# Column mean of an 8192 x 8192 matrix: the running sum moved from VectorE to TensorE, with all loads on one queue and the last two tiles in pieces

## Chip, cores, metric

One core of one Trainium2 chip (trn2). The metric is device time in microseconds (us); a profile adds the span of one profiled execution, which is about 2 us shorter. In the profile lines PE is TensorE, PEld its weight loads, DVE VectorE, ACT ScalarE, SP SyncE, q a DMA queue. A load has landed when its last part has arrived.

## The reference

```python
def setup_inputs():
    return {"x": np.random.randn(8192, 8192).astype(np.float32)}

def reference(x):
    return np.mean(x, axis=0)
```

The input is 268.4 MB, the output 32 KB.

## The kernel before

Rows are cut into 64 tiles of 128 partitions x 8192 columns. VectorE keeps a running sum of the tiles; at the end TensorE sums over the partitions with a column of 1/8192.

```python
tiles = ctx.enter_context(tc.tile_pool(name="tiles", bufs=4))
# ... (cut: other pools)
nc.vector.memset(ones, 1.0 / R)
dma_engines = [nc.sync, nc.scalar]
for b in range(nb):                                   # 64 tiles
    t = tiles.tile([P, C], fdt, tag="xtile")
    dma_engines[b % 2].dma_start(out=t, in_=xb[b])    # two queues in turn
    if b == 0:
        prev = t
    elif b == 1:
        nc.vector.tensor_add(acc, prev, t)
    else:
        nc.vector.tensor_add(acc, acc, t)
for j in range(ng):                                   # 16 blocks of 512 columns
    ps = psum.tile([1, G], fdt, tag="ps")
    nc.tensor.matmul(out=ps, lhsT=ones, rhs=acc[:, j*G:(j+1)*G], start=True, stop=True)
    nc.scalar.copy(out=out_sb[:, j*G:(j+1)*G], in_=ps)
nc.sync.dma_start(out=out, in_=out_sb[0:1, :])
```

## Time and profile before

| | before |
|---|---|
| time, median of 15 runs | 663.13 us (662.15 to 664.72) |
| span of the profiled run | 660.1 us |
| loads | 432 GB/s until about 624 us, then nothing |
| VectorE | 64 instructions, 547.7 us busy; one addition 8.69 us |
| after VectorE's last wait for a load (623.2) | 36.9 us: two additions, 16 matmuls, copy, store |

The prediction below shows the lines. They are read in two stages: as long as the DMA share is 1.00, the loads set the pace, however busy VectorE is; after that the engines work one after the other, and every microsecond counts.

### The profile page before, as it was taken

Reading aid. Unit: us, or ns where it says so; the run is one execution under the profiler, and the core shown is the slowest. Engines: PE = TensorE matmul, PEld = TensorE weight load, DVE = VectorE, ACT = ScalarE, POOL = GpSimd, SP = SyncE. Lnnn points to the kernel's source line nnn. Section 1 sums busy time; section 2 is a strip of 40 time slices with the busy share of each in tenths; the row PEclk is TensorE's granted clock in tenths of the full one; section 3 lists DMA queues with packets and bytes.
Section 4 is the critical chain, followed back from the end, with each engine's and each line's share of the span. In section 5 each row is a group of like instructions: output and inputs, shape, how many; then the busy total and the mean of one; then the engine's idle time right before and its main releaser. Section 6 shows DMA issues by size and latency. Waiting matters only on the chain.

```text
span 660.1 us, 379 instructions
## 1 busy us (share of the span) xinstructions
PE 15.6 (2%) x32; PEld 2.8 (0%) x32; DVE 547.7 (83%) x64; ACT 10.5 (2%) x17; POOL 0.2 (0%) x4
## 2 busy tenths in 40 slices
PE   0000000000000000000000000000000000000017
PEld 0000000000000000000000000000000000000001
DVE  0548999888888988888988888898888899888880
ACT  0000000000000000000000000000000000000005
POOL 0000000000000000000000000000000000000000
PEclk9999999999999999999999999999999999999999
DMA  9999999999999999999999999999999999999700
GB/s 381 439 421 443 427 431 439 421 443 425 433 439 419 445 421 437 437 421 445 415 441 437 421 445 415 443 433 425 443 415 445 429 429 439 419 445 427 338 0 2
DMA packets 9220, 268.49 MB, mean 407 GB/s; under 512 B 1025, under 2 KB 1025, under 8 KB 1025
## 3 DMA queue, kind: packets, MB, share of 16 engines
q10 hardware_dynamic: 4608, 134.22, 47.3%
q1 hardware_dynamic: 4610, 134.25, 47.3%
q14 instruction: 2, 0.02, 0.0%
HBM read 268.44 MB, written 0.03 MB: 407 GB/s over the span
## 4 chain that ended last, share of the span: by engine, by line
DMA 74%; DVE 22%; PE 2%; issue 0%; ACT 0%; SPq 0%; DVEq 0%
DMA t<-in_x_dram 74%; DVE acc L49 22%; PE ps L55 2%; ACT out_sb L62 0%; SPq L43 0%; DVEq L49 0%
## 5 line engine op out<-in xcount | busy, mean ns | idle before, releaser
L49 DVE TENSOR_TENSOR acc<-acc,t 128x8192 f32<-128x8192 f32 x62 | 538.9, 8692 | 70.3 <-DMA t<-in_x_dram 69.3
L55 PE MATMUL ps<-acc,ones 128*1 128x512 f32 x32 | 15.6, 652 | 640.7 <-DVE acc L49 640.7
L47 DVE TENSOR_TENSOR acc<-t 128x8192 f32<-128x8192 f32 x1 | 8.7, 8693 | 21.9 <-DMA t<-in_x_dram 21.9
L62 ACT ACT_TABLE_LOAD x1 | 1.3, 1283 | 602.2 <-DVE acc L49 602.2
L62 ACT COPY out_sb<-ps 1x512 f32<-1x512 f32 x16 | 9.2, 575 | 44.3 <-PE ps L55 44.3
L55 PEld LDWEIGHTS ps<-acc,ones 128*1 128x1 f32 x32 | 2.8, 89 | 652.6 <-DVE acc L49 640.7
L35 DVE MEMSET ones<- 128x1 f32 x1 | 0.1, 59 | 0.8 <-PEq L79 0.8
L79 POOL MEMSET const-uint8-127<- 128x1 uint8 x1 | 0.1, 103 | 0.0
L79 POOL MEMSET const-bfloat16-1.0<- 128x1 bf16 x1 | 0.1, 102 | 0.0
L79 POOL MEMSET const-float32-0.0<- 128x1 f32 x1 | 0.1, 99 | 0.2 <-issue 0.2
L79 POOL MEMSET const-float32-1.0<- 128x1 f32 x1 | 0.1, 99 | 0.0
## 6 DMA issues: line engine op xcount, KB each, us to landing
t<-in_x_dram ACTq DMA_DIRECT2D x32, 4096.0 KB, 26.2
t<-in_x_dram SPq DMA_DIRECT2D x32, 4096.0 KB, 30.0
out_dram<-out_sb SPq DMA_DIRECT2D x1, 32.0 KB
```

Of the source, the lines that this page charges most:

```text
L35: nc.vector.memset(ones, 1.0 / R)
L47: nc.vector.tensor_add(acc, prev, t)
L49: nc.vector.tensor_add(acc, acc, t)
L55: nc.tensor.matmul(out=ps, lhsT=ones, rhs=acc[:, j * G : (j + 1) * G], start=True, stop=True,)
L62: nc.scalar.copy(out=out_sb[:, j * G : (j + 1) * G], in_=ps)
L79: nc = _bacc.Bacc("TRN2", target_bir_lowering=False, num_devices=1)
```

## The change

The intent is to remove the serial end. TensorE adds each tile straight into PSUM accumulators as it lands, neighbouring column blocks in different column groups (strips of TensorE's array, chosen by the output's first partition, here 0 and 64) and in different banks of PSUM. All loads go on one queue. The last two tiles come in 16 pieces of 1024 columns. ScalarE and VectorE share the copies, and half of the result is stored early.

```diff
-    acc = accp.tile([P, C], fdt)
-    dma_engines = [nc.sync, nc.scalar]
-        dma_engines[b % 2].dma_start(out=t, in_=xb[b])
-            nc.vector.tensor_add(acc, acc, t)
 ... (cut)
+    NBANK = 8
+    PSPART = [0, 64, 32, 96]
+    TAIL_TILES = 2
+    DW = 1024
+    def ps_ap(j):
+        s = j % 2                       # neighbours in different column groups
+        k = (j // 2 + 4 * s) % NBANK    # and in different banks
+        p = PSPART[s]
+        return ps_tiles[k][p : p + 1, :]
 ... (cut: emit_copy: even j on ScalarE, odd j on VectorE; emit_out: store one half)
+        if b < nb - TAIL_TILES:
+            nc.sync.dma_start(out=t, in_=xb[b])
+            for j in range(ng):
+                nc.tensor.matmul(out=ps_ap(j), lhsT=ones, rhs=t[:, j * G : (j + 1) * G],
+                                 start=(b == 0), stop=(b == nb - 1))
+        else:
+            for c in range(ndw):
+                nc.sync.dma_start(out=t[:, c * DW : (c + 1) * DW],
+                                  in_=xb[b][:, c * DW : (c + 1) * DW])
 ... (cut: the same matmuls piece by piece; copies and stores in the last tile)
```

More of the change, by code (lines that the diff above doesn't have):

```diff
@@ L5 @@
 import concourse.tile as tile
-from concourse import bass_utils, mybir
+from concourse import mybir
 from concourse._compat import with_exitstack
@@ L21 @@
     nb = R // P
-    xb = x.rearrange("(b p) c -> b p c", p=P)
-    fdt = mybir.dt.float32
-    tiles = ctx.enter_context(tc.tile_pool(name="tiles", bufs=4))
-    accp = ctx.enter_context(tc.tile_pool(name="accp", bufs=1))
-    consts = ctx.enter_context(tc.tile_pool(name="consts", bufs=1))
-    outp = ctx.enter_context(tc.tile_pool(name="outp", bufs=1))
-    psum = ctx.enter_context(tc.tile_pool(name="psum", bufs=4, space=bass.MemoryType.PSUM))
-    acc = accp.tile([P, C], fdt)
+    fdt = mybir.dt.float32
@@ new lines @@
+    G = 512
+    ng = C // G
+    assert C % G == 0
+    NBANK = 8
+    nsets = (ng + NBANK - 1) // NBANK
+    PSPART = [0, 64, 32, 96]
+    assert nsets <= len(PSPART)
+    TAIL_TILES = 2
+    DW = 1024
+    ndw = C // DW
+    xb = x.rearrange("(b p) c -> b p c", p=P)
+    tiles = ctx.enter_context(tc.tile_pool(name="xt", bufs=4))
+    consts = ctx.enter_context(tc.tile_pool(name="cst", bufs=1))
+    stag = ctx.enter_context(tc.tile_pool(name="stg", bufs=1))
+    psum = ctx.enter_context(tc.tile_pool(name="ps", bufs=1, space=bass.MemoryType.PSUM))
@@ L34 @@
     ones = consts.tile([P, 1], fdt)
     nc.vector.memset(ones, 1.0 / R)
-    out_sb = outp.tile([1, C], fdt)
-    dma_engines = [nc.sync, nc.scalar]
-    prev = None
-    for b in range(nb):
-        t = tiles.tile([P, C], fdt, tag="xtile")
-        dma_engines[b % 2].dma_start(out=t, in_=xb[b])
-        if b == 0:
-            prev = t
-        elif b == 1:
-            nc.vector.tensor_add(acc, prev, t)
-        else:
-            nc.vector.tensor_add(acc, acc, t)
-    G = 512
-    ng = C // G
@@ L53 @@
-    for j in range(ng):
-        ps = psum.tile([1, G], fdt, tag="ps")
-        nc.tensor.matmul(
-            out=ps,
-            lhsT=ones,
-            rhs=acc[:, j * G : (j + 1) * G],
-            start=True,
-            stop=True,
-        )
-        nc.scalar.copy(out=out_sb[:, j * G : (j + 1) * G], in_=ps)
-    nc.sync.dma_start(out=out, in_=out_sb[0:1, :])
+    nbank_used = min(NBANK, ng)
+    ps_tiles = [
+        psum.tile([P, G], fdt, tag=f"ps{k}", name=f"ps{k}")
+        for k in range(nbank_used)
+    ]
@@ new lines, in ps_ap, with emit_copy @@
+    def ps_ap(j):
[3 more added lines that the diff above has]
+        return ps_tiles[k][p : p + 1, :]
+    set_w = nbank_used * G
+    stage = stag.tile([max(PSPART[:nsets]) + 1, set_w], fdt)
+    outv = out.rearrange("(k s g) -> s k g", s=2, g=G)
+    def emit_copy(j):
+        p = PSPART[j % 2]
+        dst = stage[p : p + 1, (j // 2) * G : (j // 2 + 1) * G]
+        if j % 2 == 0:
+            nc.scalar.copy(out=dst, in_=ps_ap(j))
+        else:
+            nc.vector.tensor_copy(out=dst, in_=ps_ap(j))
@@ new lines, in emit_out @@
+    def emit_out(h):
+        half = set_w // 2
+        for s in range(nsets):
+            p = PSPART[s]
+            eng = nc.sync if s == 0 else nc.scalar
+            eng.dma_start(
+                out=outv[s : s + 1, h * 4 : (h + 1) * 4, :],
+                in_=stage[p : p + 1, h * half : (h + 1) * half].rearrange("p (k g) -> p k g", g=G),
+            )
+    for b in range(nb):
+        t = tiles.tile([P, C], fdt, tag="xt")
+        if b < nb - TAIL_TILES:
+            nc.sync.dma_start(out=t, in_=xb[b])
+            for j in range(ng):
+                nc.tensor.matmul(
+                    out=ps_ap(j),
+                    lhsT=ones,
+                    rhs=t[:, j * G : (j + 1) * G],
+                    start=(b == 0),
+                    stop=(b == nb - 1),
+                )
+        else:
+            per = DW // G
+            for c in range(ndw):
+                nc.sync.dma_start(
+                    out=t[:, c * DW : (c + 1) * DW],
+                    in_=xb[b][:, c * DW : (c + 1) * DW],
+                )
+            for c in range(ndw):
+                for jj in range(per):
+                    j = c * per + jj
+                    nc.tensor.matmul(
+                        out=ps_ap(j),
+                        lhsT=ones,
+                        rhs=t[:, j * G : (j + 1) * G],
+                        start=(b == 0),
+                        stop=(b == nb - 1),
+                    )
+                    if b == nb - 1:
+                        emit_copy(j)
+                if b == nb - 1 and c == ndw // 2 - 1:
+                    emit_out(0)
+            if b == nb - 1:
+                emit_out(1)
```

## The prediction

> **What bounds the kernel now.** I read the profile in this order: the totals of the page, then the chain of work that ended last, then the windows, then the timeline of the last 40 us. The totals alone mislead, because they show VectorE as the busiest engine:
>
> ```profile
> span 660.1 us, 379 instructions
> PE 15.6 (2%) x32; PEld 2.8 (0%) x32; DVE 547.7 (83%) x64; ACT 10.5 (2%) x17; POOL 0.2 (0%) x4
> ...
> q10 hardware_dynamic: 4608, 134.22, 47.3%
> q1 hardware_dynamic: 4610, 134.25, 47.3%
> ...
> DMA 74%; DVE 22%; PE 2%; issue 0%; ACT 0%; SPq 0%; DVEq 0%
> ...
> L49 DVE TENSOR_TENSOR acc<-acc,t 128x8192 f32<-128x8192 f32 x62 | 538.9, 8692 | 70.3 <-DMA t<-in_x_dram 69.3
> ```
>
> VectorE is busy for 83% of the span, but the last line says that it sat idle 70.3 us in total, 69.3 of them waiting for a load of t. The two queues fill 47.3% + 47.3% = 94.6% of the 16 DMA engines' span, which is 624.5 of 660.1 us: the loads are without a pause while they last. The windows (window, length, busy time of each engine, clock, DMA share, GB/s) confirm it and show where it stops:
>
> ```profile
> 42.00:119.50 77.50, 0.00 (x0) 0.00 (x0) 71.70 (x9) 0.00 (x0) 0.00 (x0) 1.00 1.01 433
> 119.50:621.00 501.50, 0.00 (x0) 0.00 (x0) 449.60 (x52) 1.28 (x1) 0.00 (x0) 1.00 1.00 432
> ...
> 623.00:632.00 9.00, 0.00 (x0) 0.00 (x0) 8.74 (x2) 0.00 (x0) 0.00 (x0) 1.00 0.04 18
> 632.00:641.00 9.00, 0.30 (x1) 0.09 (x2) 8.65 (x1) 0.00 (x0) 0.00 (x0) 1.00 0.00 0
> 641.00:660.00 19.00, 15.34 (x32) 2.70 (x30) 0.00 (x0) 9.20 (x16) 0.00 (x0) 1.00 0.00 2
> ```
>
> So there are two stages. Up to about 624 us the kernel is bound by its loads: 432 GB/s, DMA share 1.00, and 4.19 MB / 432 GB/s = 9.71 us for one tile of 128x8192. One addition takes 8.69 us, 1 us less than a tile takes to arrive. After 624 us the DMA engines are empty and the span runs on for 36 us, one engine at a time. The chain of waits by time has it:
>
> ```profile
> 593.10 30.03 DMA t<-in_x_dram
> ...
> 623.23 8.70 DVE acc L49
> ...
> 631.96 8.70 DVE acc L49
> ...
> 640.70 15.65 PE ps L55 x32
> ...
> 656.37 0.57 ACT out_sb L62
> ```
>
> Two queues share the engines, so the last two tiles land together at 623.2: two additions in a row (17.4 us), then 16 matmuls that all need the finished sum (15.6 us), a copy (0.6), and from 656.97 to 660.1 the store and the end (3.1).
>
> **What the Trainium skill says.** (1) "FP8 and Floating Point Precision", TensorE Precision Notes: true fp32 takes four passes of the array. The trace agrees in cost: 16 matmul calls became 32 instructions with 32 weight loads, and in the timeline, from the fifth instruction on, the weight loads are 0.43 us apart (644.59, 645.01, 645.44), so one fp32 matmul of 512 columns costs 0.86 us, which is four times 512 columns at the page's 2.4 GHz, 0.853. The first four instructions were 0.85 us apart. (2) "TensorE: Matmul & The Clock Gate", Part 3: matmuls of few output columns that write different column groups, set by the output's start partition, run concurrently; three of them gave 2.38 times. The same part says that a weight load overlaps matmuls in flight only if the row group differs, and here all row groups are the same. The trace before has one column group only: it shows weight loads hidden under matmuls there, and nothing on concurrency. (3) "DMA: Bandwidth & Descriptors", Issuing engines are not separate DMA queues: queues of different engines end on the same 16 DMA engines and only save issue time. The trace agrees as far as it goes: one issue takes 0.33 us against 9.71 us of data, and between 620 and 622 us one queue held 114% of the engines' time (packets count where they start) while the other moved 0.03 MB. (4) The same page, Where 436 GB/s comes from, puts the ceiling at 435 GB/s; 432 measured, so the load stage can hardly get faster.
>
> **The change, part by part.**
>
> 1. The 63 additions (538.9 + 8.7 us of VectorE) go. They lay beside loads except for the last two, so this takes 17.4 us off the path and no more.
>
> 2. TensorE now sums every tile: 64 x 16 = 1024 fp32 matmuls. One after the other they would cost 1024 x 0.86 = 881 us, or 13.7 us a tile against 9.71 of load, and TensorE would be the bound. The change puts neighbours into column groups at partitions 0 and 64. The built program confirms tiles of 128x32 at column positions 0 and 64, alternating, in eight banks. Name a matmul's two instructions A1 A2, the next one's B1 B2. Starts are in order: A2 must follow A1 in the same group, but B1 may run beside A2, then the next C1 beside B2. A new matmul then starts each 0.43 us, 16 x 0.43 = 6.9 us a tile, under 9.71. If a weight load of 0.08 us stands exposed at each step, 16 x 0.51 = 8.2 us; if two do, 16 x 0.59 = 9.4. All three stay below 9.71, so loads stay the bound. The half-rate start (0.85 us) would cure itself, since TensorE then runs without gaps.
>
> 3. All loads go from one queue in order. The total is the same, 268.4 MB: 64 x 9.71 = 621.4 us from the first packet at about 1.2 gives 622.7, with skew of the engines some 624 to 625, as now. A tile's buffer comes free about 7 us after it lands, with three tiles (29 us) still queued, so four buffers are enough. The last two tiles come in 16 pieces of 512 KB with rows of 4 KB rather than 32 KB. Eight completion semaphores limit it to eight pieces in flight, 9.7 us of data. For the smaller rows I allow 1 us: last landing 625.5. This 1 us is a guess that the trace cannot give.
>
> 4. The end. Pieces of 512 KB land every 1.21 us, and TensorE needs 0.86 us for their two matmuls, so it is level when the last one lands. Then 3 x 0.43 (two overlapped matmuls) plus 0.17 (an instruction lasts 0.592 at a cadence of 0.43) = 1.5; a copy of 1x512 0.6, the last two now on ScalarE and VectorE side by side; signals 0.2; store and end 3.1 as measured. Sum 5.4, in place of 36. Half of the output is stored earlier, hidden.
>
> Sum: 625.5 + 5.4 = 630.9 us of span. The profiled run had 662.08 us for a span of 660.1, and the median of five is 663.32, 3.2 above the span; adding 2 to 3 gives 633 to 634. I take 633.5, that is 4.5% less.
>
> **The rivals.** (a) No concurrency: the four passes of fp32 might use the array or its read path so that two column groups cannot stream at once, or the weight loads with equal row groups might keep them apart. Then TensorE runs through, 64 x 13.7 = 878 plus 11 us for the first tile and 4 for the end: about 895 us, 35% slower. For it: the page's 2.38 names no fp32, and its remark on row groups; against it: the change arranges order, banks and partitions for just this. I give it 13%. (b) Half concurrency: A2 beside B1 works but B2 and C1 do not overlap, so a pair takes 3 x 0.43 = 1.28 us, a tile 10.2 us, slightly over 9.71. Then TensorE is the bound: 11 + 64 x 10.2 + 4 = 670 us, plus 3, within 2% of now. 6%. (c) One queue leaves gaps: if each engine pauses between two loads for the completion write, at 0.3 us a tile 19 us come back, and at 0.5 us all of the gain: 653 to 665 us. Against it stands the stretch with one queue at full rate, but it is short. 7%. (d) The small pieces are much worse than I allow, say 350 in place of 432 GB/s over 8.4 MB: 4.6 us more, 637 us; still faster.
>
> **Range and chances.** If the mechanism holds, the result should lie within 628 to 642, where the doubts are the gaps of (c) in small, (d) and the last store. Rivals (b) and (c) in full give 650 to 675, (a) 895. Faster by over 2% means below 650.1. Range 627 to 648, chances 0.79 faster, 0.09 same, 0.12 slower.
>
> **What would show it.** In the changed profile: the DMA share 1.00 and 430 to 432 GB/s to about 625 us, one queue; the chain nearly all loads of t; TensorE waiting for loads about 2 to 3 us a tile; matmul starts in pairs so that a tile's 32 instructions span 7 to 8 us; from the last landing to the end 5 to 6 us. Wrong: matmuls 0.43 us apart one by one and a span over 13 us a tile (a); TensorE waiting for nothing and the load queue waiting for TensorE (a, b); a DMA rate under 420 with TensorE idle (c).

## The result

| | before | after |
|---|---|---|
| median | 663.13 us (15 runs) | 636.77 us (8 runs, 635.63 to 636.92) |
| ratio, 95% interval | | 0.9597, 0.9588 to 0.9607 |
| span | 660.1 | 634.9 |

A ratio here is the mean time of one kernel's fast runs over that of the other's fast runs of the same rounds, so it is not quite the ratio of the medians. It says 4.0% faster; the point predicted was 633.5, the range 627 to 648. Of the eight runs two lie at 635.6 and six at 636.6 to 636.9.

The page of the changed kernel (totals, queues with packets, MB and share of the engines, chain, costliest group):

```profile
span 634.9 us, 4311 instructions
PE 484.8 (76%) x2048; PEld 90.6 (14%) x2048; DVE 5.6 (1%) x9; ACT 5.6 (1%) x9; POOL 0.2 (0%) x4
...
q1 hardware_dynamic: 11248, 268.46, 98.6%
q8 instruction: 16, 0.26, 0.2%
...
DMA 76%; PE 22%; ACT 0%; issue 0%; DVE 0%; ACTq 0%
...
L85 PE MATMUL ps<-t,ones 128*1 128x512 f32 x1984 | 471.0, 631 | 146.3 <-DMA t<-in_x_dram 146.3
```

TensorE now waits for loads, 146.3 us in all, as VectorE did before. One queue carries everything. A row is new: q8, 16 fetches of instructions, 0.26 MB, since the program grew from 379 to 4311 instructions. The windows show a load stage like that of before, and a ragged end of it:

```profile
12.00:608.00 596.00, 462.31 (x1952) 86.16 (x1952) 0.00 (x0) 0.00 (x0) 0.00 (x0) 0.95 1.00 431
...
626.00:627.00 1.00, 1.00 (x6) 0.18 (x4) 0.81 (x2) 0.72 (x2) 0.00 (x0) 1.00 0.51 209
627.00:628.00 1.00, 1.00 (x8) 0.26 (x6) 0.83 (x2) 0.72 (x2) 0.00 (x0) 1.00 0.52 213
```

431 GB/s at a share of 1.00 holds in the middle. Between 626 and 628 us the share is about one half, where in the kernel before it is 0.00 from 625 us on: half of the engines' time is still taken by loads. And TensorE, in the chain by time:

```profile
576.81 31.78 DMA t<-in_x_dram
608.59 0.04 issue
608.64 8.73 PE ps L85 x32
617.37 11.21 PE ps L102 x52
```

From 608.64 on the chain leaves the loads for good: TensorE works without a wait until 631.1. The last two tiles (L102) start when tile 61 (L85) is done, not when their pieces land. (The chain then goes by ScalarE, which issued an early store before its last four copies. They end at 631.90 and VectorE's at 631.86, so this costs nothing.)

### The profile page after: what moved, and what is told of

It is laid out like the page before. It is cut to its first block, busy times and chain, and to the rows that moved or that the text cites. A ratio compares the mean times of both kernels' runs of the same rounds, so it can differ in the third digit from the quotient of the medians.

```text
span 634.9 us, 4311 instructions
## 1 busy us (share of the span) xinstructions
PE 484.8 (76%) x2048; PEld 90.6 (14%) x2048; DVE 5.6 (1%) x9; ACT 5.6 (1%) x9; POOL 0.2 (0%) x4
## 4 chain that ended last, share of the span: by engine, by line
DMA 76%; PE 22%; ACT 0%; issue 0%; DVE 0%; ACTq 0%
DMA t<-in_x_dram 76%; PE ps L85 21%; PE ps L102 2%; ACT stage L66 0%; DVE stage L68 0%; ACTq L75 0%
## 5 line engine op out<-in xcount | busy, mean ns | idle before, releaser
L85 PE MATMUL ps<-t,ones 128*1 128x512 f32 x1984 | 471.0, 631 | 146.3 <-DMA t<-in_x_dram 146.3
L85 PEld LDWEIGHTS ps<-t,ones 128*1 128x1 f32 x1984 | 87.7, 87 | 528.7 <-issue 338.7
L102 PE MATMUL ps<-t,ones 128*1 128x512 f32 x64 | 13.9, 592 | 0.0
L68 DVE COPY stage<-ps 1x512 f32<-1x512 f32 x8 | 5.5, 689 | 625.5 <-PE ps L102 625.5
L66 ACT COPY stage<-ps 1x512 f32<-1x512 f32 x8 | 4.3, 572 | 625.6 <-PE ps L102 625.6
L102 PEld LDWEIGHTS ps<-t,ones 128*1 128x1 f32 x64 | 2.9, 84 | 10.8 <-issue 9.1
```

The lines of the kernel that those rows point to most:

```text
L66: nc.scalar.copy(out=dst, in_=ps_ap(j))
L68: nc.vector.tensor_copy(out=dst, in_=ps_ap(j))
L85: nc.tensor.matmul(out=ps_ap(j), lhsT=ones, rhs=t[:, j * G : (j + 1) * G], start=(b == 0), stop=(b == nb - 1),)
L102: nc.tensor.matmul(out=ps_ap(j), lhsT=ones, rhs=t[:, j * G : (j + 1) * G], start=(b == 0), stop=(b == nb - 1),)
```

## The experiments

Two questions: what makes the changed kernel fast, and why it came 3.3 us later than predicted. There were twelve runs, all with correct results except one that is wrong on purpose.

### 1. The last two tiles loaded whole

```diff
-            for c in range(ndw):
-                nc.sync.dma_start(out=t[:, c*DW:(c+1)*DW], in_=xb[b][:, c*DW:(c+1)*DW])
+            nc.sync.dma_start(out=t, in_=xb[b])
```

> The changed kernel with its last two tiles loaded whole (one load of 4 MB each, not 16 pieces), all else the same. Theory (the pieces buy little: they land late, about 628.3 us, because rows of 4 KB move at 400 to 410 GB/s and the DMA engines finish unevenly, and TensorE is behind anyway): the last landing comes back to about 624.5 us, then 6.9 to 8.6 us of matmuls, 0.7 for a copy and 3.0 for the store: span 635 to 637, time 637 to 639, at most 2 us slower than the changed kernel's 636.8. Rival (the pieces are what makes the end short, as the prediction had it: 1.5 us from the last landing to the last sum against 6.9): 5 us slower, 641 to 643.

Measured: 641.58 us, ratio 0.9675 (0.9656 to 0.9693). My theory of that moment was wrong and the rival right: the pieces are worth 4.8 us. The chain by time shows the last landing at 627.85, not 624.5:

```profile
596.15 31.70 DMA t<-in_x_dram
627.85 0.04 issue
627.90 6.21 PE ps L98 x20
```

So whole loads land late too, and the pieces do not cause most of the lateness. Sections 3, 4 and 6 return to this.

### 2. Order of the column groups, and one group only

```diff
-            for j in range(ng):
+            for j in [*range(0, ng, 2), *range(1, ng, 2)]:                             # same_group_order
+            for j in [0, 2, 4, 6, 1, 3, 5, 7, 8, 10, 12, 14, 9, 11, 13, 15]:           # runs_of_four
```

```diff
-    PSPART = [0, 64, 32, 96]
+    PSPART = [0, 0, 0, 0]                                                              # one_group
-        k = (j // 2 + 4 * s) % NBANK
+        k = j // 2      # blocks j and j+1 share an accumulator: wrong sums
 (start only for even j, stop only for odd j; all copies on ScalarE)
```

> The changed kernel with the matmuls of each whole tile issued first for the even and then for the odd column blocks, so that neighbours share a column group; same matmuls, same accumulators. Theory (two column groups side by side are what keeps TensorE under the load rate): a tile takes 16 x 0.86 = 13.7 us, TensorE is the bound, 62 x 13.7 + 13 + 14 + 4 = 880 us of span, 875 to 900 in time. Rival (fp32 matmuls of one column overlap whatever their group, or the order does not matter): 637.

Measured: 675.17 us, ratio 1.0179. TensorE is the bound (busy 98%), yet far from 880. The timeline of the weight loads (start, length of one, count) shows why. In the changed kernel there are two in each step of 0.43 us:

```profile
300.06 0.09 PEld L85 LDWEIGHTS ps<-t,ones 128*1 128x1 f32 x2 [0.34 <-issue]
300.49 0.09 PEld L85 LDWEIGHTS ps<-t,ones 128*1 128x1 f32 x2 [0.34 <-issue]
```

With the groups in long runs there is one in each step, but around a change of group there are 3, 2 and 2:

```profile
302.53 0.08 PEld L85 LDWEIGHTS ps<-t,ones 128*1 128x1 f32 x1 [0.34 <-issue]
302.96 0.09 PEld L85 LDWEIGHTS ps<-t,ones 128*1 128x1 f32 x3 [0.34 <-issue]
303.39 0.09 PEld L85 LDWEIGHTS ps<-t,ones 128*1 128x1 f32 x2 [0.34 <-issue]
303.82 0.09 PEld L85 LDWEIGHTS ps<-t,ones 128*1 128x1 f32 x2 [0.34 <-issue]
304.25 0.08 PEld L85 LDWEIGHTS ps<-t,ones 128*1 128x1 f32 x1 [0.34 <-issue]
```

From 302.96 to the next such place at 308.11 there are 12 steps for 16 instructions: four instructions run beside the other group's at each change. A tile takes 24 steps of 0.43 = 10.3 us. That is above 9.71, so TensorE is the bound: 13 to the first landing, 62 x 10.3, 13.8 for the two tiles in pieces (which still alternate) and 4 make 669, against a span of 672.7. Within a long run neighbours write different banks and still go one by one, so different banks alone do not make them overlap. Whether two groups would overlap in one bank was not run. To see the machine without any overlap, a second run used one group only.

> The changed kernel with every matmul in the one column group at partition 0; blocks j and j+1 then share an accumulator, so the result is wrong on purpose. The order experiment took 10.3 us a tile and not 13.7, so my number for no concurrency is untested. Theory (two instructions run together only in different column groups): one instruction each 0.43 us, 13.7 us a tile, span 13 + 64 x 13.7 + 4 = 894, time 885 to 905. Rival (instructions of one group overlap too, and that is why the order experiment was faster than 880): 640 to 680.

Measured: 899.78 us, ratio 1.3561, wrong result as intended; one weight load in each step, 13.7 us a tile. (Here neighbours also share an accumulator; the long runs above exclude that as the reason.) Overlap therefore needs different column groups, and it is worth 263 us here. A third run tested the count of four:

> The changed kernel with the matmuls of each whole tile in runs of four per column group (even blocks 0 2 4 6, odd blocks 1 3 5 7, then 8 10 12 14 and 9 11 13 15), eight instructions a run. The order experiment had runs of 16 instructions in 12 steps of 0.43 us, so four instructions overlapped at each change of group. Theory (up to four waiting instructions of one group let the other group start): a run of eight takes 8 - 4 = 4 steps, 6.9 us a tile as with alternation, load-bound, 636 to 638. Rival (the share that overlaps is a quarter whatever the run, or only neighbours overlap): 9 to 12 us a tile; at 10.3 the time is 675.

Measured: 636.51 us, ratio 0.9593, load-bound as expected, but a tile takes 8.75 us and not 6.9. The four are right, my steps were not: TensorE waits after each tile, so a tile has three changes of group, not four: 32 - 3 x 4 = 20 steps of 0.43 = 8.6 us, and 0.17 for the last instruction.

```profile
305.99 8.75 PE L85 MATMUL ps<-t,ones 128*1 128x512 f32 x32 [0.96 <-DMA t<-in_x_dram]
```

### 3. The kernel before, first with one queue, then with its last tile in pieces as well

```diff
-    dma_engines = [nc.sync, nc.scalar]
+    dma_engines = [nc.sync, nc.sync]
 (before_pieces also: the last tile in 8 loads of 1024 columns; for each piece one addition,
  then its two matmuls and copies)
```

> The kernel before with all loads on one queue, nothing else changed. Theory (one queue costs no bandwidth, and tiles land one after the other in place of in pairs, so only one addition is left after the last landing in place of two): 8.7 us less, 653.5 to 656. Rival (one queue leaves gaps between loads): DMA rate under 425 GB/s in the middle and 663 or more.

Measured: 655.81 us, ratio 0.9893 (0.9876 to 0.9909), at 432 GB/s: one queue costs no bandwidth. The chain of this run:

```profile
595.55 30.04 DMA t<-in_x_dram
...
625.68 8.71 DVE acc L49
```

VectorE's last wait ends at 625.6 and not at 623.2, 2.4 us later, and one addition of 8.7 us goes: 6.3 us, against 6.2 in the spans. The loads end no later than before: the packed traces hold for each load 16 completion events, one for each DMA engine as I read them. By these the last pair before landed at 623.14 (tile 62) and 625.56 (tile 63), and the last tile here at 625.59.

> The kernel before with one queue, its last tile loaded in 8 pieces of 512 KB, added piece by piece, each piece followed by its two matmuls and copies; the sum stays on VectorE. Theory (what the change gains is the end, not the engine of the bulk): tile 62 lands at about 615 us, then 8.7 + 8.7 us of additions end at 632 to 633, the last two matmuls 1.7 to 3.4, copy 0.6, store 3.1: span 638 to 640, time 640 to 643, most of the gain without moving the sum to TensorE. Rival (moving the sum to TensorE is needed for the gain): 653 or more.

Measured: 647.73 us, ratio 0.9768 (0.9753 to 0.9782): 5 to 8 us more than I expected. TensorE's 16 matmuls, all in one column group, cost more than the additions beside them:

```profile
624.90 1.24 DVE acc L63
626.13 0.04 issue
626.18 16.25 PE ps L69 x32
```

I had left 16 x 0.86 out. Of the gain of 26.4 us, one queue (7.5) and pieces at the end (8.1) thus come without moving the bulk of the sum. The remaining 10.9 come with the rest of the change. How they divide between the two column groups and the additions that go was not run; run 6 shows that they do not need the bulk on TensorE.

### 4. A longer program that does nothing

```diff
-    dma_engines = [nc.sync, nc.scalar]
+    dma_engines = [nc.sync, nc.sync]
+    idle = psum.tile([1, 1], fdt, tag="idle", name="idle", bufs=1)
+    for _ in range(1024):
+        nc.tensor.matmul(out=idle, lhsT=ones, rhs=ones, start=True, stop=True)
```

> The kernel before with one queue (655.8) plus 1024 idle fp32 matmuls of one column into an unused bank at its start, 4096 instructions that nothing waits for, while TensorE has nothing else to do until the end. Theory (the changed kernel's loads land 2 to 3 us late because 16 fetches of 16 KB of instructions, 1.07 us each, run on some of the same DMA engines, and a load is complete when its slowest engine is): about 16 such fetches appear, the last landing moves from 625.6 to 627.5 to 629, time 657.5 to 659.5. Rival (the late landing comes from TensorE's reads or from the order of buffers, not from the program's length): 655.8 as without them.

Measured: 657.79 us, ratio 0.9918 (0.9905 to 0.9931), 2.0 us above the same kernel without them (655.81, in another job). The page shows the same fetches as in the changed kernel, and the chain the later landing (625.6 without):

```profile
q8 instruction: 16, 0.26, 0.2%
...
597.91 30.02 DMA t<-in_x_dram
627.93 0.03 issue
```

All 16 fetches were over by 104 us, and the loads never made the time up: the last landing is 2.3 us later. The windows have the ragged end as well, a DMA share of 0.42 from 624 to 626 us where the short program has 0.00. A fetch takes about 1.07 us by the trace's records. The completion events show how this becomes 2.3 us. Of the 16 of the last load, eight come at 624.39 to 625.63 and eight at 627.56 to 627.93; without the idle matmuls all 16 come at 624.47 to 625.59. In the changed kernel, whose fetches are spread from 38 to 622 us, one more event falls some 1.5 us behind with each fetch: one by 53 us, four by 170, eight by 325. From the ninth fetch on eight fall behind a second time. So each fetch holds up one DMA engine, two fetches fall on each of eight engines, and a load lands with its slowest.

### 5. TensorE's backlog at the end

```diff
-    nsets = (ng + NBANK - 1) // NBANK
+    nsets = 4
-        s = j % 2
-        k = (j // 2 + 4 * s) % NBANK
+        s = j % 4
+        k = (j // 4 + 2 * s) % NBANK                  # four_groups (copies and stores follow)
```

```diff
-    TAIL_TILES = 2
+    TAIL_TILES = 3                                    # split_three
```

> The changed kernel with four column groups (outputs at partitions 0, 64, 32, 96) in place of two; same loads, same pieces. Theory (TensorE is one tile behind when the last pieces come, so the end waits for TensorE and not for the last landing): four groups take 16 x 0.86 / 4 = 3.4 us a tile, TensorE is level when the last piece lands at about 628.3, then about 1.1 to 1.3 to the last sum, 0.7 copy, 3.0 store: span 633 to 634, time 635 to 636, 1 to 2 us less than the changed kernel's 636.8. Rival (the end waits for the last landing already, or four groups do not run together): 636.5 to 638.

> The changed kernel with its last three tiles in pieces in place of two. Theory (the same backlog of TensorE, taken away by giving it eight more pieces to catch up, at the price of 0.45 to 0.6 us for rows of 4 KB: 161 ns each, eight of them 1288 ns against 1216 for a row of 32 KB): last landing about 628.9, span 633.5 to 634.3, time 635.4 to 636.2. Rival (no backlog): 637.2 to 637.6, later by the slower rows.

Measured: 635.52 us (0.9576, 0.9563 to 0.9589) and 636.04 us (0.9583, 0.9570 to 0.9596), both as the theory had it. Against 0.9597 (0.9588 to 0.9607) the intervals overlap, so the times alone would not settle it; the profiles do. With four groups TensorE waits for each of the last pieces and ends 1.2 us after the last landing:

```profile
621.35 7.52 DMA t<-in_x_dram
628.87 0.14 issue
629.00 1.07 PE ps L102 x4
```

The last load of the changed kernel has its last completion event at 628.92 too, and its TensorE (done at 631.1) was 1 us late. The backlog alone did not do that; see step 4 below.

### 6. Hybrids

VectorE sums the bulk as before on one queue; TensorE sums that sum and the last tiles, so the program is short.

```diff
+    PE_TILES = 10          # hybrid: two groups, last 3 tiles in pieces of 1024
+    PE_TILES = 4           # hybrid_four: four groups, last tile in 4096, 2048, 1024, 512, 512 columns
+    PE_TILES = 4           # hybrid_even: four groups, last 2 tiles in 2048, 2048, 2048, 1024, 1024
+        if b < nb - PE_TILES:                              # (cut: loads, first tile)
+            nc.vector.tensor_add(acc, prev if b == 1 else acc, t)
+        elif b < nb - TAIL_TILES:
+            if b == nb - PE_TILES:
+                sum_tile(acc, True)
+            sum_tile(t, False)
```

> VectorE sums the first 54 tiles as before, one queue; TensorE sums that sum and the last 10 tiles in two column groups as in the changed kernel; the last three tiles in pieces. Theory (short program, so hardly any instruction fetches; 24 pieces give TensorE time to catch up): last landing about 626.5 to 627 in place of 628.3, last sum 1.5 us later, copy and store 3.7: span 631.5 to 632.5, time 633.5 to 634.5, 2 to 3 us under the changed kernel. Rival (fetches do not matter and TensorE's pace at the end does not either): 636 to 638, as the changed kernel.

Measured: 634.84 us, ratio 0.9566 (0.9553 to 0.9579), below the changed kernel, a little above my range. The last landing was 628.0, not 626.5 to 627. The windows show a DMA share of 0.25 and 0.06 in the last two microseconds, so few engines are late. By the completion events three are, 1.6 to 2.1 us behind the first, two of them since the fetches at 558.6 and 591.7. The 24 pieces add about 1.7 us, as an estimate from the rows of 4 KB timed at the end of this document.

> VectorE sums the first 60 tiles; TensorE sums that sum and the last 4 tiles in four column groups; only the last tile is in pieces, of 4096, 2048, 1024, 512 and 512 columns. Theory (almost no instruction fetches, few short rows, TensorE level at the end): last landing 626 to 626.8, one matmul 1.0, copy 0.7, store 3.0: span 630.7 to 631.7, time 632.5 to 633.8, below the first hybrid's 634.8. Rival (the landing stays at 628, as in the first hybrid, whatever the pieces and the program's length): 634 to 635.

Measured: 634.42 us, ratio 0.9558, above my range. The last load's last completion event comes at 626.28, as expected, so the rival is wrong too. VectorE's timeline shows the bound, eight copies in a row after TensorE had waited for the whole of tile 62:

```profile
623.63 5.76 DVE L69 COPY stage<-ps 1x512 f32<-1x512 f32 x8 [27.61 <-PE ps L106]
```

> The second hybrid with its last two tiles in pieces of 2048, 2048, 2048, 1024 and 1024 columns in place of the last one alone. In the second hybrid the loads were done at about 626, but all sixteen copies were left for the last 5.8 us (VectorE from 623.6 to 629.4 without a pause). Theory (the end there is bound by copies that start too late, since TensorE waited for the whole of tile 62): copies spread over 617 to 628, last landing 626 to 626.6, two matmuls 1.1, copy 0.7, store 3.0: span 630.8 to 631.6, time 632.7 to 633.6. Rival (the last landing is 628 and bounds the end): 634.4 or more.

Measured: 633.86 us (633.49 to 634.51), ratio 0.9555 (0.9543 to 0.9567). This is the fastest version, 2.9 us below the changed kernel, and its interval is clear of that one's. It just missed its range. Matmuls waited 1.55 us for copies out of their banks and then ran at a clock of 0.50 until 626.8, so VectorE had four copies left in a row. They ended at 629.04, some 0.5 us later than one copy after the last matmul (627.80) would have; the last landing, 626.58, was as expected.

```profile
624.24 3.56 PE L106 MATMUL ps<-t,ones 128*1 128x512 f32 x16 [1.55 <-DVE stage L69]
```

## Why the prediction was right, and where it was off

**Loads are the bound, additions are off the path (steps 1 and 3).** Right. The DMA rate is 431 GB/s in the changed kernel and 432 before; one queue costs no bandwidth. The section cited in point (4) gives 435 GB/s for the fabric but about 358 for transfers from HBM; the 431 and 432 measured decide.

**Two column groups (step 2).** Right in size: no run shows the four passes of point (1) as such, but a matmul is two instructions of 0.43 us, and a tile takes 7.06 us at full clock (6.9 plus the last instruction's 0.17), two weight loads share each step, and nothing is exposed. So the remark on row groups quoted from the skill did not bind. Rival (a) was sized at 895 and is real where the groups are not used: 899.8. Rivals (b) and (c) were not seen. Incomplete was the picture that only neighbours in the program overlap: four instructions of one group run beside the other group's at each change.

**The last landing (step 3), predicted 625.5, measured 628.9.** This is the larger miss. Loads land at 625.6 with a short program, 1.1 us more than the 624.5 from which I started. That was a misreading of the kernel before: its last two tiles do not land together at 623.2. Tile 63 lands at 625.56 and VectorE needs it only at 631.96. The pieces cost 1.1 (628.92 against 627.85), by luck close to the 1 us that was called a guess. The missing term is the fetch of the longer program, 2.3 us by the idle-matmul run. 1.1 + 2.3 makes the 3.4.

**"It is level when the last one lands" (step 4), predicted 1.5 us from the last landing to the last sum, measured 2.2** (628.9 to 631.1). I compared the rates of a piece, 0.86 against 1.21, and forgot where TensorE stood at the start: tile 61 comes whole, so at 608.64 three tiles of work lie ahead, 3 x 6.9 = 20.6 us. Loads are left for 20.3, and the last piece needs 1.2 after it lands, so at full clock TensorE would just have been level. But tile 61 fell into a spell of lower clock (8.73 in place of 7.06): 22.3 us, and TensorE is done 1.0 late. So what failed is the remark in step 2 that the half rate "would cure itself, since TensorE then runs without gaps". It had gaps of 2.7 us, and at least 20 of the 62 whole tiles took 8.4 to 8.7 us. Two of the eight runs have spans of 633.8 and 633.9, 0.9 to 1.3 below the other six, which would fit an end without such a spell; their traces were not kept, so this is not shown. With the backlog gone the end takes 1.2 us.

**Copy, store, and time above span.** Predicted 0.8 + 3.1, measured 3.8 together (631.1 to 634.9). Time above span was 1.9, not 2 to 3.

The sum in spans: 630.9 + 3.4 + 0.7 - 0.1 = 634.9. The gain of 26.4 us came where the prediction said, at the end: the last landing moved from 625.6 to 628.9, but what follows it shrank from 34.5 to 6.0 us. The pieces it relied on are needed: whole tiles give 4.8 us back.

## What to carry to other kernels

When loads already run at full rate, look at what follows the last landing, and count what each engine has left to do when the last whole tile arrives, not only its rate per piece. Here sixteen matmuls of one output row cost 13.7 us in one column group, 7.06 in two and 3.61 in four (the hybrids), when neighbours alternate; in runs of 8 instructions per group they took 8.75, in runs of 16 10.3. Count the instructions that a change adds: their fetches use the engines that carry the loads, so keep the bulk on an engine that needs few, and spend TensorE on the end.

## What the Trainium skill lacked or had wrong

- "Runtime: NRT & Kernel Launch", Instruction fetch mechanics, says that fetches come in blocks of 16 KiB (256 instructions) and that crossing a boundary is "mostly hidden". The count agrees: 16 fetches for 4096 TensorE instructions. Saturated loads did not hide them: each set one DMA engine back by some 1.5 us, and the last landing moved by 2.3 us (625.6 to 627.9).
- "TensorE: Matmul & The Clock Gate", Part 3, gives column tiling without fp32 and without order. Here fp32 matmuls (two instructions of 0.43 us each) overlap in two groups (6.9 us for 16, against 13.7 in one), and four instructions overlap at each change of group.
- The same part says that a weight load overlaps matmuls in flight only if the row group differs. With equal row groups and different column groups, two weight loads and two matmuls shared each 0.43 us step; even in one group the weight load of 0.08 us lay inside the step.
- The same page, Why this matters for your kernels, puts the harmful idle gap of TensorE at over about 3 us. Gaps of 2.7 us were enough here for a mean clock of 0.945 and tiles of 8.73 us in place of 7.06. With four groups, gaps of 3.1 to 5.7 us gave 0.759, which cost nothing under the loads.
- "DMA: Bandwidth & Descriptors", Specifications, calls transfers of 512 B and up enough for line rate. Rows of 4 KB took 161 ns each, so eight take 1288 against 1216 for one row of 32 KB: 6% slower, 1.1 us over the last two tiles.
